# First feed-forward feature pair in plain products for both token halves, with split weight parts stored once and loaded for the second half

## The chip, the cores and the metric

The kernel runs on one core of a Trainium2 chip. The metric is the device time of one execution in microseconds. The kernel before takes 2255.2 us (median of three runs, 2255.18 to 2257.11).

## The reference

One decoder layer on 1024 tokens of 1024 features, in fp32: an mLSTM and a differential attention side by side, then cross-attention into 256 memory tokens, then a SwiGLU feed-forward with 2816 hidden features. Each sub-layer ends in x <- LayerNorm(alpha * x + f(x)). The change touches the end of the second sub-layer and the start of the third:

```python
    p = jax.nn.softmax(s, axis=-1)
    xo = jnp.einsum('bhqk,bkhd->bqhd', p.astype(xv.dtype), xv).reshape(B, S, XA_HEADS * XA_DHEAD)
    x = layer_norm(ALPHA * x + xo @ w_xo[l], ln2_g[l], ln2_b[l])

    hid = jax.nn.silu(x @ w_ffn_gate[l]) * (x @ w_ffn_up[l])
    x = layer_norm(ALPHA * x + hid @ w_ffn_down[l], ln3_g[l], ln3_b[l])
```

## The kernel before, in words

**Products.** Every fp32 operand is split into a high part (`whi`) and a remainder (`wlo`), and each product is three matmuls, high by high, high by low, low by high (`mm3`). A weight comes by DMA on SP's queue into `wraw` (three buffers); a high part is then a copy by ScalarE (ACT) or GpSimd (POOL), a low part a subtraction by VectorE (DVE) or POOL (`split_w`). `whi` and `wlo` have four buffers each, so four parts of 128 by 512 stand ready at a time. `turn` decides the engine: without a plan high parts alternate between ACT and POOL, and of four low parts three go to DVE and one to POOL.

**Order.** `Weave` runs generators one quantum at a time, and TensorE's order is the order in which they are stepped (one quantum of the attention output or of a plain product is six matmuls of 256 columns, or a few more). Work that must wait for LayerNorm is put in a heap by `W.later` and comes due after so many quanta. The other engines' order comes from a scheduler that goes by priority: `tc.high_priority(offset=AHEAD)` lets weight loads and splits stand ahead of other work. Once set, each engine's order is fixed and it waits in order.

**The stretch of the change.** The attention output and its LayerNorm (`g_add`) run once for the first 512 tokens (h = 0) and once for the last 512 (h = 1). Each half goes through four column quarters b, and each quarter through two units u of 256 tokens; a unit is eight quanta. Each quarter loads 1 MB of weights (`vo_d[b]`, two loads) and splits it into four parts, in each half anew. At quarter 3 each token tile of 128 rows gets its LayerNorm; in h = 1 POOL takes half of the last two steps of it (`LN2_POOL`).

`to_blocks(h, p)` then transposes two token tiles into PSUM tiles `tp` (a pool of five banks, four needed at once) and makes from them the blocks `x2[h]` of the feed-forward's input: four plain blocks and three or four sums and differences, each with a high and a low part. The gate and up products of a pair of feature blocks (q) use seven half-size products in place of eight (`g_seven`, Strassen's scheme in Winograd's form), so they need the sums and differences of the input and also those of the weights (`tt` on DVE). For the first pair (q = 0) the token halves differ: h = 0 is done by `g_seven` on 256 columns, as soon as its blocks are there; h = 1 is done by `g_plain`, eight products from plain blocks, while `block_sums` makes its sums from the plain blocks. From q = 1 on both halves go together through `g_seven`.

Of the kernel before, what the change touches and what calls it, by code (L numbers as in the profile page):

```python
# [12 lines left out]
F = mybir.dt.float32  # L13
R = mybir.dt.float32r
# [9 lines left out]
KT = 8  # L24
# [92 lines left out]
def hybrid_layer(ctx: ExitStack, tc: tile.TileContext, a: dict, out: bass.AP):  # L117
# [86 lines left out]
    def g_tm(wsrc, nk, units, evac):  # L204

        w = []
        for g0 in range(0, nk, 4):
            gn = min(4, nk - g0)
            w += split_all(load_w(wsrc[:, g0:g0 + gn, :]), gn * 256)
# [35 lines left out]
    hT_d = dr.tile([2, 8, 128, 1024], F, name="hT_d")  # L245
    oT_d = dr.tile([8, 128, 1024], F, name="oT_d")
# [711 lines left out]
    def g_add(wsrc, act, h, b, gb, dst=None):  # L958
# [12 lines left out]
        yield from g_tm(wsrc, KT, half(act), ev)  # L971
# [78 lines left out]
    def to_blocks(h, p):  # L1050
# [32 lines left out]
    def block_sums(p, late):  # L1083

        c = slice(p * 128, p * 128 + 128)

        def part(n, i):
            return x2[1][i][n][:, :, c].bitcast(F)

        t, u = diff_tile(), diff_tile()  # L1090
        if late:
            tt(t, part(3, 0), part(0, 0), OP.subtract)
            tt(u, part(3, 1), part(0, 1), OP.subtract)
            tt(t, t, u, OP.add)
            put(1, 3, c, t, "g")
            return
        tt(t, part(2, 0), part(3, 0), OP.subtract)
        tt(u, part(2, 1), part(3, 1), OP.subtract)
        tt(t, t, u, OP.add)
        put(1, 5, c, t, "g")  # L1100
        tt(u, t, part(0, 0), OP.add)
        tt(u, u, part(0, 1), OP.add)
        put(1, 4, c, u, "g")
        t = diff_tile()
        tt(t, part(1, 0), u, OP.subtract)
        tt(t, t, part(1, 1), OP.add)
        put(1, 6, c, t, "v")

    def g_sums(late):
        for p in range(2):  # L1110
            block_sums(p, late)
        yield from ()
# [320 lines left out]
```

## Time and profile before

| | |
|---|---|
| median of three runs | 2255.2 us |
| profiled execution | 2254.51 us |
| its span in the trace | 2252.6 us |
| TensorE busy | 2192.5 us (97%) |
| VectorE busy | 1386.7 us (62%) |
| ScalarE, GpSimd busy | 695.2 us, 709.7 us |
| HBM read, written | 168.92 MB, 41.98 MB |

The trace's times are microseconds from the span's start. A matmul's busy time is longer than the distance to the next one, since matmuls are pipelined: what counts is where one group starts and the next one starts. In brackets behind a row stands how long its engine was idle before it and what ended that. PEclk is TensorE's granted clock, 1.00 for 2.4 GHz and 0.50 for 1.2 GHz, as a mean over the stretch.

### The profile page before, as it was taken

How to read it: one execution, taken by the hardware profiler on the slowest of the kernel's cores; microseconds unless marked ns; L12 is line 12 of the kernel's file. 1: busy time of each engine (PE TensorE's matmuls, PEld its weight loads, DVE VectorE, ACT ScalarE, POOL GpSimd, SP SyncE). 2: the span in 40 equal slices, each digit the busy share in tenths (PEclk: the TensorE clock that was granted, in tenths of full speed). 3: DMA queues.
4: the chain of work that ended last, by engine and by line, in shares of the span. 5: the costliest groups of instructions: out<-in, count | busy, mean ns of one | idle time of the engine just before them, and what ended most of it. 6: DMA issues, size and time to landing. Idle time of an engine off the chain costs nothing.

```text
span 2252.6 us, 34100 instructions
## 1 busy us (share of the span) xinstructions
PE 2192.5 (97%) x13149; PEld 1953.5 (87%) x13149; DVE 1386.7 (62%) x2494; ACT 695.2 (31%) x1395; POOL 709.7 (32%) x723
## 2 busy tenths in 40 slices
PE   8999999999999999998999999997999999999997
PEld 8898898888898988886888999997888888888886
DVE  8536545314777777765535586478756666565667
ACT  3323223213555555555212123222211111111122
POOL 7124323203334343434422232245421121111223
PEclk9999999999999999999999999999999999999999
DMA  9322212334434454338653423222211111111122
GB/s 323 102 75 94 75 66 94 117 110 120 117 93 140 124 148 129 101 117 287 215 178 122 178 85 104 83 83 70 66 40 55 50 45 57 57 57 39 56 80 80
DMA packets 97953, 238.33 MB, mean 106 GB/s; under 512 B 12128, under 2 KB 30464, under 8 KB 97792
## 3 DMA queue, kind: packets, MB, share of 16 engines
q1 hardware_dynamic: 97792, 236.16, 32.1%
q8 instruction: 104, 1.70, 0.3%
q14 instruction: 57, 0.47, 0.1%
HBM read 168.92 MB, written 41.98 MB: 94 GB/s over the span
## 4 chain that ended last, share of the span: by engine, by line
PE 45%; DVE 4%; POOL 1%; issue 1%; ACT 0%; DMA 0%; DVEq 0%; POOLq 0%; ACTq 0%
PE acc L153 27%; PE xb L153 7%; PE xa L153 5%; PE xc L153 5%; DVE wlo L150 1%; DVE d L1039 1%; DVE z L929 0%; DVE z L925 0%; PE tp L1002 0%; DVE wraw L1039 0%; DVE u L1039 0%; DVE lst L935 0%; DVE xb L150 0%; PE tp L953 0%; DVE hidl L150 0%
## 5 line engine op out<-in xcount | busy, mean ns | idle before, releaser
L153 PE MATMUL acc<-bh,whi 128*128 128x512 f32 x2048 | 649.3, 398 | 0.4 <-ACT gtok L392 0.4
L142 POOL TENSOR_SCALAR whi<-wraw 128x512 fp32r<-128x512 f32 (+1 forms) x250 | 180.9, 724 | 889.2 <-issue 382.7
L153 PEld LDWEIGHTS acc<-bh,whi 128*128 128x128 f32 x2048 | 372.2, 188 | 65.7 <-ACT gtok L392 0.6
L150 DVE TENSOR_TENSOR wlo<-wraw,whi 128x512 fp32r<-128x512 f32 (+1 forms) x379 | 310.4, 823 | 189.9 <-ACT whi L140 148.8
L153 PE MATMUL acc<-bh,wlo 128*128 128x512 f32 x1024 | 400.3, 391 | 0.0
L140 ACT ACTIVATE whi<-wraw 128x512 fp32r<-128x512 f32 (+1 forms) x252 | 157.3, 625 | 553.5 <-PE acc L153 279.8
L153 PE MATMUL acc<-whi,bh 128*128 128x256 f32 (+1 forms) x1456 | 288.1, 288 | 0.2 <-DVE ev L150 0.2
L153 PEld LDWEIGHTS acc<-whi,bh 128*128 128x128 f32 x1456 | 234.2, 191 | 1.5 <-DVE ev L150 0.4
L153 PEld LDWEIGHTS acc<-bh,wlo 128*128 128x128 f32 x1024 | 192.3, 188 | 42.1
L153 PE MATMUL acc<-wlo,bh 128*128 128x256 f32 (+1 forms) x728 | 205.5, 282 | 0.0
L153 PE MATMUL xb<-xe,whi 128*128 128x256 f32 x1008 | 183.7, 282 | 10.7 <-DVE u L1039 7.8
L150 POOL TENSOR_TENSOR wlo<-wraw,whi 128x512 fp32r<-128x512 f32 (+1 forms) x125 | 174.6, 1397 | 10.3
L153 PEld LDWEIGHTS xb<-xe,whi 128*128 128x128 f32 x1008 | 160.3, 190 | 15.9 <-issue 6.7
L153 PE MATMUL xb<-xe,wlo 128*128 128x256 f32 x504 | 142.7, 283 | 0.0
L153 PEld LDWEIGHTS acc<-wlo,bh 128*128 128x128 f32 x728 | 138.8, 191 | 1.1
L1254 DVE SCALAR_TENSOR_TENSOR z<-z,acc 128x512 f32<-128x512 f32 x144 | 98.3, 685 | 53.7 <-PE acc L153 52.5
L153 PE MATMUL acc<-wlo,hidh 128*128 128x512 f32 x320 | 124.8, 390 | 1.4 <-DVE wlo L150 1.4
L153 PE MATMUL acc<-whi,hidh 128*128 128x512 f32 x320 | 124.6, 389 | 1.2 <-POOL whi L142 1.2
L153 PE MATMUL acc<-whi,hidl 128*128 128x512 f32 x320 | 124.7, 390 | 0.0
L688 ACT ACTIVATE e<-e,mx 128x256 f32<-128x256 f32 (+7 forms) x128 | 99.2, 775 | 73.5 <-DVE mx L683 71.8
L153 PE MATMUL xa<-xb,whi 128*128 128x512 f32 (+1 forms) x352 | 106.6, 386 | 5.3 <-ACT u L1166 5.3
L153 PE MATMUL xc<-xb,whi 128*128 128x512 f32 (+1 forms) x352 | 105.8, 383 | 1.6 <-DVE u L1039 1.6
(297 smaller groups left out, 4344.7 us busy)
## 6 DMA issues: line engine op xcount, KB each, us to landing
wraw<-in_wfm_dram SPq DMA_DIRECT2D x48, 512.0 KB, 3.5
wraw<-in_wg_dram SPq DMA_DIRECT2D x24, 512.0 KB, 3.5
wraw<-in_wu_dram SPq DMA_DIRECT2D x24, 512.0 KB, 3.5
wraw<-in_wd_dram SPq DMA_DIRECT2D x22, 512.0 KB, 3.5
hT_d<-hp SPq DMA_DIRECT2D x16, 512.0 KB, 2.8
g_d<-gt SPq DMA_DIRECT2D x32, 256.0 KB, 2.1
K<-rot SPq DMA_DIRECT2D x64, 128.0 KB, 2.4
klo<-raw SPq DMA_DIRECT2D x64, 128.0 KB, 2.4
```

What stands on the lines that cost most here:

```text
L140: S.activation(dst, src, AF.Copy)
L142: G.tensor_scalar(dst, src, 1.0, 0.0, op0=OP.mult, op1=OP.add)
L150: (V if eng == "v" else G).tensor_tensor(dst, src, hi.bitcast(F), op=OP.subtract)
L153: PE.matmul(o, l, r, start=start, stop=stop, skip_group_check=True)
L688: S.activation(e[c][:, :n], e[c][:, :n], AF.Exp, scale=-1.0, bias=mx[:, c:c + 1], accum_out=su[:, c:c + 1])
L1039: V.tensor_tensor(dst, x_, y_, op=op)
L1254: V.scalar_tensor_tensor(zs, zs, ALPHA if q == 0 else 1.0, acc, op0=OP.mult, op1=OP.add)
```

## The change

The attention output's first half stores the split parts of its weights to memory (`vs_d`), and its second half loads these parts straight into `whi` and `wlo`; it splits nothing. For q = 0 both token halves now use `g_plain`: h = 0 splits the weights and stores the parts (`pl_d`), h = 1 loads them. `to_blocks` makes six of the seven blocks for either half; while the plain products run, block 6 holds a plain block, and `g_sums` puts the seventh sum there when they are done. In this whole stretch all high parts of weights are made by ACT (`turn["plan"] = ("s", None)`).

```diff
-    def g_tm(wsrc, nk, units, evac):
-
-        w = []
-        for g0 in range(0, nk, 4):
-            gn = min(4, nk - g0)
-            w += split_all(load_w(wsrc[:, g0:g0 + gn, :]), gn * 256)
+    def load_parts(src):
+
+        hi = wp.tile([128, 512], R, tag="whi", name="whi", bufs=4)
+        lo = wp.tile([128, 512], R, tag="wlo", name="wlo", bufs=4)
+        with tc.high_priority(offset=AHEAD):
+            dma(hi.bitcast(F), src[0])
+            dma(lo.bitcast(F), src[1])
+        return hi, lo
+
+    def g_tm(wsrc, nk, units, evac, parts=None, again=False):
+
+        if again:
+            w = [load_parts(parts[i]) for i in range(4)]
+        else:
+            w = []
+            for g0 in range(0, nk, 4):
+                gn = min(4, nk - g0)
+                w += split_all(load_w(wsrc[:, g0:g0 + gn, :]), gn * 256)
+            if parts is not None:
+                for d, pair in zip(parts, w):
+                    for j in range(2):
+                        dma(d[j], pair[j].bitcast(F))
...
-        if h == 1:
-            for n, b in enumerate((b11, b21, b22, b12)):
-                put(1, n, c, b, "v")
-            return
-        put(0, 0, c, b11, "v")
-        t1 = diff_tile()
+        for n, b in ((0, b11), (1, b21)):
+            put(h, n, c, b, "v")
+        t1, t3 = diff_tile(), diff_tile()
         S.activation(t1, b12, AF.Copy)
-        t3 = diff_tile()
+        put(h, 6, c, b12, "v")
+        put(h, 2, c, b22, "v")
         tt(t3, b22, t1, OP.subtract)
         tt(t1, t1, b11, OP.subtract)
-        put(0, 5, c, t3, "g")
-        put(0, 1, c, b21, "v")
-        put(0, 3, c, t1, "g")
+        put(h, 5, c, t3, "g")
         t2 = diff_tile()
         tt(t2, b22, t1, OP.subtract)
-        put(0, 2, c, b22, "v")
-        put(0, 4, c, t2, "g")
-        t4 = diff_tile()
-        tt(t4, b21, t2, OP.subtract)
-        put(0, 6, c, t4, "g")
...
+        put(h, 3, c, t1, "g")
+        put(h, 4, c, t2, "g")
+
+    def g_sums(h):
...
+            t, u = diff_tile(), diff_tile()
+            tt(t, part(1, 0), part(4, 0), OP.subtract)
+            tt(u, part(1, 1), part(4, 1), OP.subtract)
             tt(t, t, u, OP.add)
-            put(1, 3, c, t, "g")
...
+            put(h, 6, c, t, "g")
         yield from ()
 
     gb2 = ln_rows(1)
+    turn["plan"] = ("s", None)
...
-    def g_plain(wsrc, f, up):
-
-        w = split_all(load_w(wsrc[f]))
+    def g_plain(wsrc, f, up, h):
+
+        kept = pl_d[2 * up + f]
+        if h == 0:
+            w = split_all(load_w(wsrc[f]))
+            for d, pair in zip(kept, w):
+                for j in range(2):
+                    dma(d[j], pair[j].bitcast(F))
+        else:
+            w = [load_parts(d) for d in kept]
...
-    W.add("g", g_gate_up(0, [0], False))
-    W.add("u", g_gate_up(0, [0], True))
-    W.add("g", g_plain(a["wg"], 0, False))
-    W.add("g", g_plain(a["wg"], 1, False))
-    W.add("s", g_sums(False))
-    W.add("u", g_plain(a["wu"], 0, True))
-    W.add("u", g_plain(a["wu"], 1, True))
-    W.add("s", g_sums(True))
+    for h in range(2):
+        for up in range(2):
+            for f in range(2):
+                W.add("p", g_plain(a["wu" if up else "wg"], f, up, h))
+        W.add("s", g_sums(h))
+    W.drain()
+    turn["plan"] = None
```

The first place is SP's queue from the attention output on. In the kernel before it holds the 16 loads of `vo_d` (both halves) and then loads of feed-forward weights:

```order
L167 DMA wraw<-vo_d 128x1024 x16
L167 DMA wraw<-in_wg_dram 128x1024 x2
L167 DMA wraw<-in_wu_dram 128x1024 x2
L167 DMA wraw<-in_wg_dram 128x1024 x2
L167 DMA wraw<-in_wu_dram 128x1024 x2
```

In the changed kernel the first half's loads stand among the stores of the parts, of which this is a stretch (`vs_83` and `vs_84` are parts 0 and 1 of quarter 2):

```order
L167 DMA wraw<-vo_d 128x1024
L225 DMA vs_83<-whi 128x512
L225 DMA vs_83<-wlo 128x512
L225 DMA vs_84<-whi 128x512
L167 DMA wraw<-vo_d 128x1024
L225 DMA vs_84<-wlo 128x512
```

The second half's queue then starts like this (`vs_75` to `vs_78` are the four parts of quarter 0):

```order
L167 DMA wraw<-in_wg_dram 128x1024
L167 DMA wraw<-in_wu_dram 128x1024
L210 DMA wlo<-vs_75 128x512
L209 DMA whi<-vs_75 128x512
L209 DMA whi<-vs_76 128x512
L210 DMA wlo<-vs_76 128x512
L209 DMA whi<-vs_77 128x512
L210 DMA wlo<-vs_77 128x512
```

A store of a part stands behind the split that makes it, a load of a part waits until TensorE has done with the part that has held its buffer, and what stands behind either on SP waits too. Eight loads of 256 KB take the place of two of 512 KB in each quarter of the second half.

The second place is DVE where the last token tile (`z7`) has its LayerNorm and the last blocks are made. In the kernel before:

```order
L925 SCALAR_TENSOR_TENSOR z7_12157<-z7_12157,lmv_15753,lng_14578 128x512 x2
L929 SCALAR_TENSOR_TENSOR z7_12157<-z7_12157,lrs_15759,lnb_14579 128x512
L150 TENSOR_TENSOR wlo_16116<-wraw_16113,whi_16115 128x512
L150 TENSOR_TENSOR wlo_16120<-wraw_16113,whi_16119 128x512
L150 TENSOR_TENSOR hidl_15773<-sg_15854,hidh_15772 128x2x128
L150 TENSOR_TENSOR xb_14576<-tp_15977,xb_14574 128x4x128
L1039 TENSOR_TENSOR u3_16035<-xb_15950,u1_15964 128x256
L150 TENSOR_TENSOR xb_14576<-tp_15987,xb_14574 128x4x128
L1039 TENSOR_TENSOR u3_16035<-xc_15951,u3_16035 128x256
L150 TENSOR_TENSOR xb_14576<-tp_15982,xb_14574 128x4x128
L1039 TENSOR_TENSOR u3_15868<-u3_15868,u3_16035 128x256
```

And in the changed kernel:

```order
L943 SCALAR_TENSOR_TENSOR z7_12181<-z7_12181,lmv_15789,lng_14602 128x512 x2
L150 TENSOR_TENSOR wlo_16050<-wraw_16047,whi_16049 128x512
L947 SCALAR_TENSOR_TENSOR z7_12181<-z7_12181,lrs_15795,lnb_14603 128x512
L150 TENSOR_TENSOR wlo_16054<-wraw_16047,whi_16053 128x512
L1057 TENSOR_TENSOR s1_16424<-wraw_16422 128x512
L150 TENSOR_TENSOR xb_14600<-tp_15961,xb_14598 128x4x128
L150 TENSOR_TENSOR xb_14600<-tp_15966,xb_14598 128x4x128
L1057 TENSOR_TENSOR wraw_16422<-wraw_16420,wraw_16422 128x512
L150 TENSOR_TENSOR xe_15807<-tp_15971,xe_15806 128x4x128
L150 TENSOR_TENSOR xb_14600<-tp_15976,xb_14598 128x4x128
L1057 TENSOR_TENSOR d_15986<-tp_15976,d_15985 128x512
L1057 TENSOR_TENSOR d_15985<-d_15985,tp_15961 128x512
```

The combining of the seven products (`u1` to `u3`) is gone from between the blocks. The row that ends the fence is the last reader of the first transposed tile `tp_15961`; until then that tile's PSUM bank is taken.

The third place is TensorE in the last plain call of h = 0, with the transposes of tiles 6 and 7, one quantum into the call:

```order
L153 MATMUL acc<-xb,whi 128x256 x2
L153 MATMUL acc<-xb,wlo 128x256
L153 MATMUL acc<-xe,whi 128x256 x2
L153 MATMUL acc<-xe,wlo 128x256
L1076 MATMUL tp<-ident,z_12180 128x128 x8
L1076 MATMUL tp<-ident,z_12181 128x128 x8
L153 MATMUL acc<-xb,whi 128x256 x2
```

The transposes of tiles 4 and 5 stand one quantum into the call before. In the kernel before both pairs of tiles come among the seven-product calls.

## Rows read from the trace of the kernel before

**Rows 1.** The page's first part: busy time, share of the span, instructions.
```profile
PE 2192.5 (97%) x13149; PEld 1953.5 (87%) x13149; DVE 1386.7 (62%) x2494; ACT 695.2 (31%) x1395; POOL 709.7 (32%) x723
```

**Rows 2.** Windows: length, busy us (instructions) by engine, granted clock, DMA share, GB/s.
```profile
1544.20:1551.80 7.60, 6.04 (x37) 5.85 (x37) 6.06 (x10) 0.05 (x1) 5.72 (x6) 0.78 0.44 140
1560.90:1570.60 9.70, 3.11 (x25) 2.94 (x25) 9.70 (x15) 1.05 (x2) 8.17 (x7) 0.89 0.44 155
1570.60:1577.47 6.87, 6.87 (x40) 6.87 (x41) 6.29 (x13) 3.44 (x6) 0.00 (x0) 0.66 0.04 13
1577.47:1600.51 23.04, 23.04 (x194) 23.04 (x193) 22.77 (x29) 7.70 (x14) 11.90 (x9) 1.00 0.21 69
1600.51:1611.53 11.02, 5.75 (x38) 5.05 (x36) 9.83 (x12) 2.27 (x4) 7.20 (x6) 0.90 0.01 1
1611.53:1616.53 5.00, 5.00 (x13) 3.96 (x13) 2.89 (x4) 0.00 (x0) 1.46 (x3) 0.53 0.06 8
```

**Rows 3.** TensorE's timeline: start, length, operation, idle before it and its releaser.
```profile
1536.89 0.40 PE L153 MATMUL xa<-xb,whi 128*128 128x256 f32 x2
...
1544.20 0.52 PE L153 MATMUL xb<-xe,whi 128*128 128x256 f32 x2 [2.86 <-POOL whi L142]
...
1570.60 0.76 PE L153 MATMUL xb<-xe,whi 128*128 128x256 f32 x2 [6.56 <-DVE u L1039]
1572.01 3.48 PE L1058 MATMUL tp<-ident,z 128*128 128x128 f32 x16
...
1600.51 0.63 PE L153 MATMUL xa<-xb,whi 128*128 128x512 f32 x2
...
1611.53 1.22 PE L153 MATMUL xa<-xb,whi 128*128 128x512 f32 x2 [5.27 <-ACT u L1166]
...
1627.73 0.39 PE L153 MATMUL acc<-whi,hidh 128*128 128x512 f32 x1
```

**Rows 4.** TensorE's timeline: sixteen transposes and what follows them.
```profile
1502.03 1.91 PE L1058 MATMUL tp<-ident,z 128*128 128x128 f32 x16
1503.69 0.36 PE L153 MATMUL acc<-whi,pt 128*128 128x256 f32 x1
```

**Rows 5.** The chain of waits in order of time: two products of a seven-product call.
```profile
1616.69 2.84 PE xb L153 x24
1619.53 2.76 PE xc L153 x12
```

**Rows 6.** TensorE's timeline: gaps in the attention output's second half.
```profile
1497.65 0.39 PE L153 MATMUL acc<-wlo,pt 128*128 128x256 f32 x1 [0.62 <-DVE wlo L150]
...
1511.49 0.63 PE L1058 MATMUL tp<-ident,z 128*128 128x128 f32 x4 [0.50 <-DVE xb L150]
```

**Rows 7.** DVE's instructions by form, 1538.2 to 1627.7: busy us, mean ns, idle before.
```profile
L150 DVE TENSOR_TENSOR wlo<-wraw,whi 128x512 fp32r<-128x512 f32 x20 | 17.5, 881 | 5.4 <-POOL whi L142 3.3 <-ACT whi L140 2.1
L150 DVE TENSOR_TENSOR xb<-tp,xb 128x512 fp32r<-128x512 f32 x8 | 5.4, 674 | 0.3 <-ACT xb L140 0.2
L964 DVE SCALAR_TENSOR_TENSOR z<-z,acc 128x256 f32<-128x256 f32 x2 | 0.7, 364 | 0.0
L936 DVE BATCH_NORM_AGGREGATE lmv<-lst 128x2 f32<-128x12 f32 x3 | 0.6, 198 | 0.0
```

**Rows 8.** POOL's instructions by form, 1531 to 1570.
```profile
L945 POOL TENSOR_TENSOR z<-z,lnb 128x512 f32<-128x512 f32 x4 | 5.7, 1436 | 0.3
L944 POOL TENSOR_SCALAR z<-z,lrs 128x512 f32<-128x512 f32 x4 | 5.4, 1362 | 2.3 <-DVE z L925 2.3
L920 POOL TENSOR_TENSOR lrs<-lsc,mhalf 128x1 f32<-128x1 f32 x4 | 4.0, 990 | 11.9 <-DVE lsc L938 11.9
```

**Rows 9.** DMA issues: count, KB each, median us from issue to landing.
```profile
bh<-hT_d SPq DMA_DIRECT2D x16, 512.0 KB, 7.4
wraw<-vo_d SPq DMA_DIRECT2D x16, 512.0 KB, 3.7
```

**Rows 10.** SP's timeline: eight of the `hT_d` loads.
```profile
1042.00 7.76 SPq L820 DMA_DIRECT2D bh<-hT_d  x8
```

**Rows 11.** Windows: the ten us that hold these loads, columns as in the second group.
```profile
1042.00:1052.00 10.00, 6.75 (x27) 5.46 (x26) 4.93 (x14) 5.43 (x12) 2.92 (x4) 0.83 1.05 397
```

More of the change, by code (lines that the diff above doesn't have):

```diff
@@ L245, in hybrid_layer @@
     hT_d = dr.tile([2, 8, 128, 1024], F, name="hT_d")
+    vs_d = [[dr.tile([2, 128, 512], F, name=f"vs{b}{i}") for i in range(4)] for b in range(4)]
+    pl_d = [[dr.tile([2, 128, 512], F, name=f"pl{b}{i}") for i in range(2)] for b in range(4)]
     oT_d = dr.tile([8, 128, 1024], F, name="oT_d")
@@ L956, in to_feature, with g_add @@
             to_lo(dst[1][:, 4 * g:4 * g + 4, c], t3, dst[0][:, 4 * g:4 * g + 4, c], "v")
-    def g_add(wsrc, act, h, b, gb, dst=None):
+    def g_add(wsrc, act, h, b, gb, dst=None, parts=None):
         def ev(u, acc):
@@ L970, in ev @@
                         W.later(LAG_B[u] if h else LAG_B0, lambda: to_blocks(h, u))
-        yield from g_tm(wsrc, KT, half(act), ev)
+        yield from g_tm(wsrc, KT, half(act), ev, parts, parts is not None and h == 1)
     gb1 = ln_rows(0)
@@ L1109, in g_sums, with part @@
-    def g_sums(late):
-        for p in range(2):
-            block_sums(p, late)
+        put(h, 3, c, t1, "g")
+        put(h, 4, c, t2, "g")
+    def g_sums(h):
+        for p in range(2):
+            c = slice(p * 128, p * 128 + 128)
+            def part(n, i):
+                return x2[h][i][n][:, :, c].bitcast(F)
+            t, u = diff_tile(), diff_tile()
+            tt(t, part(1, 0), part(4, 0), OP.subtract)
+            tt(u, part(1, 1), part(4, 1), OP.subtract)
+            tt(t, t, u, OP.add)
+            put(h, 6, c, t, "g")
@@ L1112, in g_sums @@
         yield from ()
     gb2 = ln_rows(1)
+    turn["plan"] = ("s", None)
     for b in range(4):
-        W.add(f"o0{b}", g_add(vo_d[b], pT[0], 0, b, gb2))
+        W.add(f"o0{b}", g_add(vo_d[b], pT[0], 0, b, gb2, None, vs_d[b]))
     W.drain()
     for b in range(4):
-        W.add(f"o1{b}", g_add(vo_d[b], pT[1], 1, b, gb2))
+        W.add(f"o1{b}", g_add(vo_d[b], pT[1], 1, b, gb2, None, vs_d[b]))
     W.drain()
@@ L1220, in g_plain @@
             for t in range(2):
-                n = ((0, 3), (1, 2))[k // 4][t]
+                n = ((0, 6), (1, 2))[k // 4][t]
                 mm3(acc[:, t * 256:(t + 1) * 256], cut(w[k // 4], (k % 4) * 128, (k % 4) * 128 + 128),
-                    (x2[1][0][n][:, k % 4, :], x2[1][1][n][:, k % 4, :]), k + t == 0, k == 7)
+                    (x2[h][0][n][:, k % 4, :], x2[h][1][n][:, k % 4, :]), k + t == 0, k == 7)
             yield
-        if not up:
-            sg[f] = temp("sg")
-            S.activation(sg[f], acc, AF.Silu)
-            return
-        st = sg[f]
-        tt(st, st, acc, OP.mult)
-        s4 = st.rearrange("p (t q r) -> p t q r", t=2, r=128)
-        d = [x_[:, f, 512:].rearrange("p (q t r) -> p t q r", t=2, r=128) for x_ in hid]
-        to_hi(d[0], s4, "g")
-        to_lo(d[1], s4, d[0], "v")
+        with tc.high_priority(offset=AHEAD_U):
+            if not up:
+                sg[f] = temp("sg")
+                S.activation(sg[f], acc, AF.Silu)
+                return
+            st = sg[f]
+            tt(st, st, acc, OP.mult)
+            s4 = st.rearrange("p (t q r) -> p t q r", t=2, r=128)
+            d = [x_[:, f, h * 512:h * 512 + 512].rearrange("p (q t r) -> p t q r", t=2, r=128) for x_ in hid]
+            to_hi(d[0], s4, "s")
+            to_lo(d[1], s4, d[0], "v")
     def down_w(q):
```

20 lines of the change are left out of this document (removed).

## The prediction

> **What bounds the kernel now.** I read the page's busy times first. TensorE is busy 97% of the span [rows 1], so a gain can only come from places where it stands still, runs slowly or does work that can go. A list of its idle gaps then shows the large ones in one place, the start of the feed-forward: TensorE's timeline there has it idle for 2.86, 6.56 and 5.27 us at a time [rows 3], with smaller gaps between, and the windows show after each of the large ones a granted clock below 1.00 (0.78, 0.66 and 0.53 as a mean, so partly at 1.2 GHz) while it is busy again [rows 2]. In the same windows DVE is busy 9.70 of 9.70, 22.77 of 23.04 and 9.83 of 11.02 us [rows 2]. TensorE waits for DVE, or for ACT and POOL work that DVE feeds. So this stretch is bound by VectorE, and only there does DVE work cost time.
>
> How much is lost is measured against TensorE's own pace. In the plain products of h = 1, without a gap, 192 matmuls of 256 columns (four calls of 48) go by in the 23.04 us from 1577.47 to 1600.51 [rows 2, 3], which is 0.120 us each. Sixteen transposes take 1503.69 - 1502.03 = 1.66 us [rows 4]. A product of 512 columns in a seven-product call takes 2.76 us, and 2.84 where it is cut into 256-column pieces [rows 5].
>
> The first pair before (1536.89 to 1600.51): 63.62 us [rows 3]. Its work is 2 x 84 matmuls for h = 0 (seven products, four k, three matmuls) and 192 for h = 1, 360 x 0.120 = 43.2 us, and 2 x 1.66 us of transposes: 46.5 us. So 17.1 us are lost.
> The next gate call (1600.51 to 1627.73): 27.22 us [rows 3] for 4 x 2.76 + 3 x 2.84 = 19.6 us of work: 7.6 us lost, through the 5.27 us gap and the slow clock after it.
> The attention output's second half loses 0.62 + 0.50 = 1.1 us in its two gaps [rows 6].
>
> **The change part by part.**
>
> TensorE's work grows. Both halves need 192 plain matmuls, 384 x 0.120 = 46.1 us, with the transposes 49.4 us in place of 46.5: 2.9 us more, and this lies fully on the path.
>
> DVE's work shrinks. A 512-column operation takes 0.674 us and a 256-column one 0.364 us when nothing disturbs it [rows 7]. In the attention output's second half 16 low parts go, three of four from DVE: 12 x 0.674, 8 us. In the first pair two calls of seven products go: two weight combinations of four operations each (5.4 us), 14 low parts, ten or eleven of them DVE's (7.1 us), ten operations that combine products (3.6 us) and eight that make the four 256-column results of the up call (2.9 us). Two more up evictions of two operations come (2.7 us); the plain splits stay eight, since h = 1 loads its parts. That is 16 us less, and the blocks take 20 operations a pair of tiles in place of 22 over both halves, 2.7 us less. With 19 us less in a stretch where DVE was full, it need not hold TensorE all along. If the losses vanish altogether, the gain is 63.6 - 49.4 = 14.2 us in the first pair, 7.6 in the next gate call and 1.1 in the attention output: 22.9 us. That is the ceiling.
>
> Residual wait at the last blocks. In the new order tiles 4 and 5 are transposed 17 quanta into the first pair and tiles 6 and 7 after 25. Counted from the end of the first unit of quarter 3 (5.76 us, 48 x 0.120, ahead of the first pair), TensorE reaches the latter at 5.76 + 25 x 0.72 + 1.66 = 25.4 us, and after four transposes, 0.4 us, needs a PSUM bank that the first pair of tiles still holds (five banks, four used) until DVE has done the last row of the second place shown. Up to that row DVE has 32 operations of 512 columns at about 0.68 us [rows 7] and 12 short ones (four at 0.364, four at 0.198, four below): 21.8 + 3.0 = 24.8 us. POOL works beside it nearly all that time (four LayerNorm halves at 1.436 + 1.362 and 0.990 [rows 8], 15 us, and two low parts), and two-input DVE operations were longer beside POOL: a low part took 0.881 us as a mean against 0.674 for one from PSUM [rows 7], 30% more, which would make it 32 us. So the wait is between 25.8 - 24.8, below zero, thus nothing, and 32 - 25.8 = 6 us. At the far end, if DVE is no earlier than now, the transposes come 1572.01 - 1536.89 = 35.1 us after the first pair's start [rows 3] where they now want 19.7: 15 us. I take 3 us, the middle of the nearer two ends, and 1 us for a slower clock after it (after the 2.86 us gap, 7.60 us ran at 0.78 [rows 2], 0.22 x 7.60 = 1.7 us lost). What stands behind: ACT waits in order at the block that goes where the LayerNorm's rows lie until POOL has done tile 7, and with it the eviction of the first up product; its accumulator is needed two calls later, so that is covered by 5 us and more.
>
> The parts' loads in the attention output's second half. A part is freed in unit 1 of a quarter after its two quanta and is wanted again in unit 0 of the next; for each of the four parts that is 5.76 - 1.44 = 4.32 us later. What fills it now is a split on ACT and DVE from a weight that is there already; then it is two DMAs of 256 KB. A 512 KB load from the same scratch lands 3.7 us after its issue [rows 9], and SP's second issue comes some 0.4 us later: 4.1 us against 4.32. The next pair is asked for 1.44 us later, 0.52 MB in 1.44 us or 364 GB/s while it lasts, and eight `hT_d` loads of 512 KB with the same 2 KB rows, issued one after another in 7.76 us [rows 10], ran at 397 GB/s [rows 11]. So they just fit. Bounds: nothing, since 4.1 is below 4.32, and, if each pair lands as the `hT_d` loads did in the median, 7.4 us [rows 9], 3.1 us in each of four quarters, 12.3 us. I take 0.3 us a quarter, 1.2 us, being nearest to the 3.7 us row.
>
> The Trainium skill speaks against such small transfers. Its page "DMA: Bandwidth & Descriptors", section Bandwidth, advises to batch transfers to 1 MiB or more for three quarters of the peak, and gives 358 GB/s as a core's limit from HBM. The trace differs in both: 512 KB transfers in a row ran at 397 GB/s [rows 11]. By that limit of the Trainium skill's page a quarter's 2.1 MB would take an estimated 5.9 us where they are asked for in 5.76, 0.1 us more a quarter, and the sum would be 2237.4.
>
> The rest costs nothing here. The second half of q = 0 loads its parts with a ring of four buffers, each part freed 2.88 us into a call and its buffer wanted two calls later, 2 x 5.76 - 2.88 = 8.64 us, twice the time above. The 32 and 16 stores (256 KB each) stand on SP ahead of later weight loads; each waits for a split that TensorE needs anyway some us later, and the weight loads behind are needed a quarter (11.5 us) or a call (5.76 us) later. High parts go from POOL to ACT, which was busy 7.70 of 23.04 us [rows 2]; without that cover a high part costs 0.6 us once per quarter. The seventh sums come while the next gate call runs its first five products (some 14 us), on a DVE that is then free.
>
> Sum, against the profiled execution: 22.9 - 4 - 1.2 = 17.7 us off 2254.5 gives 2236.8; the median of the runs shown lies 0.7 us above that execution, so 2237 to 2238. I forecast 2237.
>
> **The rivals.**
> 1. The blocks of h = 1 stay late. LayerNorm, blocks and POOL work for h = 1 are untouched and now stand right before the plain products of h = 1, which need them at once; before, the whole of h = 0's seven products lay between. For it: POOL's 15 us and DVE's order. Against: 19 us less on DVE. If half of the 15 us above is waited, 7.5 with 2 us of clock, in place of 4: 2237 + 5.5 = 2243; with all 15 us and 3 of clock, 2251.
> 2. Slower: the parts' loads go one after another. SP has one queue, each load waits for a buffer, and if each pair takes its 3.7 us alone [rows 9], four need 14.8 us from 7.2 us into a quarter, 22.0; the last is wanted at 11.52 + 4.32 = 15.8. That is 6.2 us a quarter, 25 in four, and 1.7 us of clock each, 32 in place of 1.2: 2237 + 31 = 2268. It decides from about 4.5 us per quarter on, which eats the 18 us. Against it stands the 397 GB/s of eight loads in a row [rows 11]. The Trainium skill's page "DMA: Bandwidth & Descriptors" (section Bandwidth) leads the same way with its advice against small transfers; the rows so far are against it.
> 3. The loads overlap but land as late as the `hT_d` median: 12.3 us and some clock, 2237 + 12 = 2249 to 2252.
> 4. Nothing waits: the ceiling, 2254.5 - 22.9 + 0.7 = 2232.
>
> **How the numbers follow.** Forecast (2234 to 2241) 0.50; rival 1 0.22; rival 4 0.13; rival 3 0.08; rival 2 0.07. A measurement of this kernel tells 0.2% (4.5 us) from no change. Faster by more than that is below 2250.7: the forecast, rival 4, nearly all of rival 1 and half of rival 3, 0.89. Within: 0.05. Slower: most of rival 2, 0.06. The range from 2231 (the ceiling with a little more) to 2250 leaves out rival 2 and the ends of 1 and 3, and holds some 0.85.
>
> **What would show it.** In the profile after, the first pair should start within 1.5 us of 1536.9 and take some 53 us from its first matmul to the first of q = 1, with DVE no longer at 95% and more; the gap of 6.56 us and the 5.27 us gap should be gone, and the next gate call should take under 21 us. A wait of some 3 us should stand at the transposes of tiles 6 and 7, released by a DVE block operation. In the attention output's second half gaps released by loads of parts should sum to about 1 us and the DMA rate should be about twice what it was. I am wrong if such gaps reach several us per quarter, if the first plain call of h = 1 waits for blocks by more than 5 us, or if the time lies above 2250.

## The result, and the profile after

The changed kernel takes 2231.8 us (median of four runs, 2231.03 to 2232.62) against 2255.45 us for the kernel before on the same chip (2255.18 to 2257.11): ratio 0.9896, 95% interval 0.9885 to 0.9908. The forecast was 2237 us, the range 2231 to 2250. The profiled execution takes 2231.29 us, its span is 2229.3 us.

The page's first part, answering [rows 1]:

```profile
PE 2187.3 (98%) x13173; PEld 1950.3 (87%) x13173; DVE 1343.7 (60%) x2446; ACT 695.7 (31%) x1392; POOL 677.6 (30%) x688
```

TensorE executes 24 matmuls more and is busy 5.2 us less, since less of its work runs at the slow clock; and it stands idle for 42.0 us of the span in place of 60.1.

TensorE's timeline at the first pair, answering [rows 3] (start, length, operation, idle before it and its releaser):

```profile
1537.78 0.40 PE L153 MATMUL acc<-xb,whi 128*128 128x256 f32 x2
...
1557.36 1.47 PE L1076 MATMUL tp<-ident,z 128*128 128x128 f32 x12
...
1559.76 0.63 PE L1076 MATMUL tp<-ident,z 128*128 128x128 f32 x4 [0.93 <-DVE d L1057]
...
1566.09 0.39 PE L153 MATMUL acc<-xe,whi 128*128 128x256 f32 x1 [0.23 <-DVE xe L150]
...
1588.75 0.63 PE L153 MATMUL xa<-xb,whi 128*128 128x512 f32 x2
...
1608.30 0.39 PE L153 MATMUL acc<-whi,hidh 128*128 128x512 f32 x1
```

The first pair takes 1588.75 - 1537.78 = 50.97 us (before 63.62), the gate call behind it 1608.30 - 1588.75 = 19.55 us (before 27.22). Of the gaps of 2.86, 6.56 and 5.27 us none is left; the two waits above, 1.16 us in sum, are all of more than 0.15 us in the two stages.

The windows of the same stretch, answering [rows 2], same columns; the first is the attention output's second half:

```profile
1490.00:1537.78 47.78, 46.58 (x387) 45.93 (x386) 26.31 (x51) 10.80 (x19) 12.13 (x11) 1.00 0.46 150
1537.78:1549.90 12.12, 12.12 (x105) 12.12 (x103) 12.09 (x24) 5.06 (x8) 10.41 (x9) 1.00 0.89 282
1549.90:1557.36 7.46, 7.46 (x67) 7.46 (x65) 7.46 (x9) 3.14 (x6) 4.67 (x4) 1.00 0.87 297
1557.36:1566.09 8.73, 7.56 (x64) 7.15 (x63) 6.65 (x11) 4.92 (x9) 3.83 (x3) 1.00 0.48 172
1566.09:1588.75 22.66, 22.66 (x188) 22.66 (x189) 15.94 (x22) 7.20 (x12) 10.27 (x8) 1.00 0.36 116
1588.75:1608.30 19.55, 19.55 (x123) 17.53 (x121) 10.04 (x14) 5.20 (x9) 6.59 (x7) 1.00 0.18 55
```

VectorE is still full, 12.09 of 12.12 and 7.46 of 7.46 us, at the start of the pair, but TensorE is busy all of these 19.58 us: of what VectorE makes there, its plain products need only the low parts of weights (the transposes at 1549.90, of tiles 4 and 5, need the LayerNorm of these). Over the whole pair VectorE is busy 42.14 of 50.97 us (the sum of the four rows of the pair). The kernel before, over its pair:

```profile
1536.89:1600.51 63.62, 51.37 (x394) 50.52 (x393) 59.46 (x89) 20.64 (x38) 36.85 (x31) 0.92 0.20 67
```

So VectorE has 17.3 us less to do in the pair. The granted clock is 1.00 in all six rows after.

Where the 23.3 us of span come from, each stage from its marks in TensorE's timeline:

| stage (us) | before | after | gain |
|---|---|---|---|
| attention output, both halves | 98.60 | 98.93 | -0.33 |
| first pair | 63.62 | 50.97 | 12.65 |
| gate call of q = 1 | 27.22 | 19.55 | 7.67 |
| from there to the last down products | 566.74 | 566.75 | -0.01 |
| last down products | 48.46 | 45.36 | 3.10 |
| behind the last matmul | 9.67 | 8.89 | 0.78 |

The rest, -0.6, is ahead of the attention output. The last two lines, 3.9 us together, stand in no term of the prediction: they lie 570 us behind the change. TensorE before, where the last down products begin:

```profile
2197.86 0.51 PE L153 MATMUL acc<-whi,hidh 128*128 128x512 f32 x1 [1.19 <-POOL whi L142]
2199.78 0.75 PE L153 MATMUL acc<-wlo,hidh 128*128 128x512 f32 x1 [1.42 <-DVE wlo L150]
```

and after:

```profile
2178.87 0.50 PE L153 MATMUL acc<-wlo,hidh 128*128 128x512 f32 x1 [1.39 <-POOL wlo L150]
```

One wait of 1.39 us in place of two with 2.61. The windows of the 39.5 us behind them show the rest, a granted clock of 0.96 before

```profile
2200.50:2240.00 39.50, 39.50 (x170) 32.57 (x169) 28.24 (x76) 12.22 (x19) 15.87 (x20) 0.96 0.20 76
```

and 1.00 after:

```profile
2179.50:2219.00 39.50, 39.50 (x176) 32.72 (x175) 29.92 (x81) 12.95 (x20) 16.45 (x21) 1.00 0.20 77
```

The same length of time holds 176 and not 170 matmuls. The wait of 1.42 us comes from VectorE's order before:

```profile
2195.55 1.78 DVE L150 TENSOR_TENSOR xe<-wraw,xe 128x512 fp32r<-128x512 f32 x1
2197.25 1.09 DVE L1039 TENSOR_TENSOR u<-u,u 128x512 f32<-128x512 f32 x1
2198.26 0.68 DVE L1039 TENSOR_TENSOR u<-xc,u 128x512 f32<-128x512 f32 x1
2198.86 0.87 DVE L150 TENSOR_TENSOR wlo<-wraw,whi 128x512 fp32r<-128x512 f32 x1
```

The low part that TensorE needs stands behind two sums of the last up products. In the changed kernel POOL makes it.

### The profile page after: what moved, and what is told of

It reads as the page before. It is cut to its first block, busy times and chain, and to the rows that moved or that the text cites. A ratio compares the mean times of both kernels' runs of the same rounds, so it can differ in the third digit from the quotient of the medians.

```text
span 2229.3 us, 34179 instructions
## 1 busy us (share of the span) xinstructions
PE 2187.3 (98%) x13173; PEld 1950.3 (87%) x13173; DVE 1343.7 (60%) x2446; ACT 695.7 (31%) x1392; POOL 677.6 (30%) x688
## 4 chain that ended last, share of the span: by engine, by line
PE 47%; DVE 2%; DMA 1%; issue 0%; POOL 0%; ACT 0%; SPq 0%; DVEq 0%; POOLq 0%; ACTq 0%
PE acc L153 29%; PE xb L153 8%; PE xc L153 5%; PE xa L153 5%; DMA wlo<-vs 1%; DVE z L947 0%; PE tp L1020 0%; DVE z L943 0%; PE tp L971 0%; DVE wlo L150 0%; PE tp L1076 0%; DVE xb L150 0%; DVE lst L953 0%; DVE s L1057 0%; POOL wlo L150 0%
## 5 line engine op out<-in xcount | busy, mean ns | idle before, releaser
L142 POOL TENSOR_SCALAR whi<-wraw 128x512 fp32r<-128x512 f32 (+1 forms) x224 | 160.8, 718 | 842.8 <-issue 334.9
L150 DVE TENSOR_TENSOR wlo<-wraw,whi 128x512 fp32r<-128x512 f32 (+1 forms) x358 | 286.0, 803 | 192.7 <-ACT whi L140 154.2
L150 POOL TENSOR_TENSOR wlo<-wraw,whi 128x512 fp32r<-128x512 f32 (+1 forms) x118 | 165.7, 1404 | 50.4 <-ACT whi L140 41.2
L153 PE MATMUL xb<-xe,whi 128*128 128x256 f32 x960 | 173.0, 280 | 0.0
L153 PEld LDWEIGHTS xb<-xe,whi 128*128 128x128 f32 x960 | 151.7, 188 | 4.7
L153 PE MATMUL xb<-xe,wlo 128*128 128x256 f32 x480 | 135.1, 281 | 0.0
L153 PE MATMUL xc<-xb,whi 128*128 128x512 f32 x320 | 99.3, 391 | 0.0
L153 PE MATMUL xa<-xb,whi 128*128 128x512 f32 x320 | 98.9, 390 | 0.0
```

The costliest lines, as they stand in the source:

```text
L142: G.tensor_scalar(dst, src, 1.0, 0.0, op0=OP.mult, op1=OP.add)
L150: (V if eng == "v" else G).tensor_tensor(dst, src, hi.bitcast(F), op=OP.subtract)
L153: PE.matmul(o, l, r, start=start, stop=stop, skip_group_check=True)
```

## The experiments

Twelve kernels in three batches, each batch on one chip with the kernel before beside it (2254.73, 2255.5 and 2255.8 us). Profiled executions differ by up to 4 us already ahead of the attention output, so below 2 us I go by stages. `turn["h"]` and `turn["l"]` count the splits and decide whose turn the next one is; where an experiment changes their number, the line `turn["h"], turn["l"] = 0, 2` ahead of the last down weights sets the counters to what the changed kernel has there (its own values, taken as turns). In the expectations theory D says that the first pair is bound by VectorE and that relieving it is the gain; theory R says that the gain at the end of the kernel comes from shifted turns.

**Which part of the change it is.** The feed-forward part alone (high parts by ACT now from the first pair on):

```diff
-    turn["plan"] = ("s", None)
...
-        W.add(f"o0{b}", g_add(vo_d[b], pT[0], 0, b, gb2, None, vs_d[b]))
+        W.add(f"o0{b}", g_add(vo_d[b], pT[0], 0, b, gb2))
...
-        W.add(f"o1{b}", g_add(vo_d[b], pT[1], 1, b, gb2, None, vs_d[b]))
+        W.add(f"o1{b}", g_add(vo_d[b], pT[1], 1, b, gb2))
...
+    turn["plan"] = ("s", None)
```

> The changed kernel without its attention-output part: both halves split the weights anew and nothing is stored; the feed-forward part stays, with its stored parts, and the counters at the end are those of the changed kernel. Theory D (VectorE held TensorE only after the attention output, so what is saved inside it brings nothing): 2231 to 2234. Rival (the 8 us of VectorE and the POOL work saved in the second half let its LayerNorm and blocks start earlier, and that is part of the gain): 2236 to 2242.

Measured 2229.6 us (0.9889, 0.9874 to 0.9904); first pair 50.96, gate call 19.54, attention output 97.44. The time is below both expectations: all of the gain is there, and the attention output is 1.5 us shorter than with the stored parts. The attention-output part alone, in the kernel before (the helpers that store and load, as in the change, are left out here):

```diff
...
-        W.add(f"o0{b}", g_add(vo_d[b], pT[0], 0, b, gb2))
+        W.add(f"o0{b}", g_add(vo_d[b], pT[0], 0, b, gb2, None, vs_d[b]))
...
-        W.add(f"o1{b}", g_add(vo_d[b], pT[1], 1, b, gb2))
+        W.add(f"o1{b}", g_add(vo_d[b], pT[1], 1, b, gb2, None, vs_d[b]))
```

> The kernel before with the attention-output part alone (stored parts, high parts by ACT); first pair as before, counters at the end as in the changed kernel. Theory D: like the kernel before with the new counters, 2250 to 2252.5. Rival: 2244 to 2249.

Measured 2249.58 us (0.9981, 0.9972 to 0.9991), with the pair at 63.34 and the gate call at 27.08 us as before. It has the changed counters, and with these alone (below) the kernel before takes 2250.92 us. So this part brings nothing that these times tell from nothing; its attention output takes 99.12 us (98.60 before). The time lies between the two expectations. No stored part at all: to the edit of the feed-forward run comes

```diff
-        if h == 0:
-            w = split_all(load_w(wsrc[f]))
...
-        else:
-            w = [load_parts(d) for d in kept]
+        w = split_all(load_w(wsrc[f]))
```

> The changed kernel without any stored part: attention output splits anew in both halves, and so do the plain calls. What is left of the change is that both halves' first feature pair runs in plain products, with seven or fewer blocks a half due ahead of them. Theory D with the attention part worth nothing: the sum of the run without the attention part (2229.6) and of what the plain splits cost (0 to 3 us): 2229.5 to 2233. Rival (stored parts are needed for the plain order to pay): 2238 or more, with DVE full through the whole pair.

Measured 2231.3 us (0.9897, 0.9882 to 0.9912), the first expectation. The pair takes 50.16 us, less than with stored parts, and VectorE is still busy 16.3 us less in it than in the kernel before:

```profile
1536.64:1586.80 50.16, 49.62 (x419) 49.40 (x418) 43.17 (x67) 23.57 (x42) 30.45 (x24) 1.00 0.26 85
```

The gate call takes 21.42 us, more, through one wait for ACT's copy of the first product. Ahead of this copy in ACT's order stand a block of the seventh sums, for which ACT first waits 4.57 us until VectorE has its sum, a hidden block and a high part:

```profile
1594.15 0.72 PE L153 MATMUL xa<-xb,whi 128*128 128x512 f32 x2 [1.61 <-ACT u L1161]
```

The same with the attention output's stored parts left in (only the edit just shown):

> The changed kernel, but the second half's four plain calls load the raw weights and split them anew, and nothing of them is stored. Theory D (DVE is full from 1537.8 to 1557.4, 19.6 of 19.6 us, so any operation put there delays the blocks that the transposes of tiles 6 and 7 wait for): 4 of the 8 low parts fall to DVE at 0.7 to 0.9 us each, two of them into the full stretch, so the pair stage takes 52 to 54 us instead of 51.0 and the time is 2232.5 to 2234.5. Rival (the second half's calls have slack, DVE 15.9 of 22.7 us, and the stored parts are not needed): pair stage within 0.5 us of 51.0, time 2231 to 2232.

Measured 2233.15 us (0.9906, 0.9892 to 0.9919). That is within the time of theory D, but not by its reason: the pair is 50.17 us, with no wait at the transposes (one of 0.54 us for a low part), and the gate call has the same 1.61 us wait (21.42 us). VectorE's timeline without stored parts shows why the low part that now stands ahead of the last blocks costs nothing there:

```profile
1555.48 0.68 DVE L1057 TENSOR_TENSOR d<-tp,d 128x512 f32<-128x512 f32 x1
1556.08 0.68 DVE L150 TENSOR_TENSOR wlo<-wraw,whi 128x512 fp32r<-128x512 f32 x1
1556.67 0.68 DVE L1057 TENSOR_TENSOR d<-d,tp 128x512 f32<-128x512 f32 x1
...
1581.64 0.68 DVE L1057 TENSOR_TENSOR s<-wraw 128x512 f32<-128x512 f32 x1
1582.36 0.69 DVE L1057 TENSOR_TENSOR wraw<-wraw 128x512 f32<-128x512 f32 x1
```

The two sums of the next gate call's weights (`s`, `wraw`), which the changed kernel does ahead of these blocks, went some 28 us back: their weights are loaded only from 1570.23 on (1544.65 in the changed kernel), behind the raw weights of the second half's plain calls, which need the same three buffers. So the wait left the pair and came up in the gate call.

By stages, the stored parts of the plain calls are worth 1.1 us (pair and gate call together 70.5 us with them and 71.6 without, in both comparisons), and those of the attention output cost 1.5 us there. The 20 us are those of plain products for both halves. These bring several things at once: TensorE has work that doesn't wait for the late blocks, VectorE has 16 to 17 us less to do in the pair, and POOL makes no high parts of their weights. No run parts them. The next one shows that the order alone is not enough.

**What bounds the pair.** Work put back on VectorE (16 low parts of the first half's plain calls made over again), without any other edit to the pair:

```diff
-            w = split_all(load_w(wsrc[f]))
+            raw = load_w(wsrc[f])
+            w = split_all(raw)
+            with tc.high_priority(offset=AHEAD):
+                for j, pair in enumerate(w):
+                    for _ in range(2):
+                        to_lo(pair[1], raw[:, j * 512:j * 512 + 512], pair[0], "v")
```

> The changed kernel with 16 low-part subtractions of the first half's plain calls done twice more on DVE (values unchanged, about 0.88 us each, 14 us of DVE work). Theory D (the pair is bounded by DVE's blocks, which is what the change relieved): what does not fit into DVE's idle time ahead of the pair comes back as waits at the transposes of tiles 6 and 7, pair stage 57 to 63 us, time 2237 to 2244. Rival (the gain came from the order of TensorE's calls alone, DVE has room): pair stage within 1 us of 51.0, time 2231 to 2233.

Measured 2244.63 us (0.9955, 0.9942 to 0.9969), a pair of 64.34 us, 13.4 longer, both a little more than theory D had. VectorE is busy 51.29 us in it, 9.15 more than in the changed kernel. Eleven low parts run in one go there from 1539.29 on, 8.21 us, ahead of the LayerNorm of the last tiles, and POOL's half of the LayerNorm is late with it. TensorE's waits of more than 0.2 us sum to 9.9 us, 8.7 more than in the changed kernel; 7.7 of them are at the transposes, now of both pairs of tiles, and 2.2 at low parts:

```profile
1555.74 0.66 PE L1076 MATMUL tp<-ident,z 128*128 128x128 f32 x4 [1.25 <-POOL z L963]
...
1563.09 0.39 PE L153 MATMUL acc<-xb,wlo 128*128 128x256 f32 x1 [1.45 <-DVE lsc L956]
...
1567.62 1.09 PE L1076 MATMUL tp<-ident,z 128*128 128x128 f32 x4 [3.36 <-POOL z L963]
...
1570.21 1.08 PE L1076 MATMUL tp<-ident,z 128*128 128x128 f32 x4 [1.50 <-DVE xe L150]
...
1572.60 1.08 PE L1076 MATMUL tp<-ident,z 128*128 128x128 f32 x4 [1.30 <-DVE d L1057]
```

The remaining 4.6 of the 13.4 us go with the clock, 0.92 where the changed kernel has 1.00:

```profile
1539.11:1603.45 64.34, 54.45 (x418) 52.42 (x417) 51.29 (x79) 20.89 (x34) 30.30 (x23) 0.92 0.46 156
```

So VectorE work that is put ahead of the LayerNorm and the last blocks costs about its own length, and the clock on top: with the plain order too, VectorE's time up to the last block is the bound, and the changed kernel has little room left in it. The rival, the order alone, falls.

One thing stays open. In the kernel before, VectorE itself waits for POOL where the first gaps are:

```profile
1541.71 0.69 DVE L150 TENSOR_TENSOR wlo<-wraw,whi 128x512 fp32r<-128x512 f32 x1 [1.77 <-POOL whi L142]
...
1549.50 0.69 DVE L150 TENSOR_TENSOR wlo<-wraw,whi 128x512 fp32r<-128x512 f32 x1 [1.54 <-POOL whi L142]
```

POOL makes the first of these high parts behind its half of a LayerNorm, and the gap of 2.86 us ends with another. All runs with plain products for both halves also have the weights' high parts on ACT. What that alone would do for the kernel before was not run.

**How tight the loads are.** Each part in two transfers, cut by columns:

```diff
-            dma(hi.bitcast(F), src[0])
-            dma(lo.bitcast(F), src[1])
+            for t, d in ((hi, src[0]), (lo, src[1])):
+                for c in (slice(0, 256), slice(256, 512)):
+                    dma(t[:, c].bitcast(F), d[:, c])
```

> The changed kernel with each stored part loaded in two transfers of 128 KB instead of one of 256 KB, so four instead of two for a pair of parts. If a load has to land within the 4.32 us that one group of four products of the attention output leaves it, and the number of transfers on the SP queue sets when it lands, the two waits for low parts (0.20 and 0.96 us) grow to 3 to 6 us in sum: 2233 to 2237. If the bytes set it, the halves land as the wholes did: waits within 1 us of before, 2231 to 2232.5.

Measured 2250.76 us (0.998, 0.9972 to 0.9989): 19 us lost, more than either expectation. In the profile the attention output takes 117.79 us, 18.86 more than in the changed kernel: 13.7 us of it are waits, the rest goes with a granted clock of 0.90 from the first of them on. TensorE waits once in each quarter of the second half:

```profile
1488.16 0.58 PE L153 MATMUL acc<-wlo,pt 128*128 128x256 f32 x1 [3.99 <-DMA wlo<-vs]
...
1507.56 0.58 PE L153 MATMUL acc<-wlo,pt 128*128 128x256 f32 x1 [5.12 <-DMA wlo<-vs]
...
1525.36 0.38 PE L153 MATMUL acc<-wlo,pt 128*128 128x256 f32 x1 [1.07 <-DMA wlo<-vs]
...
1541.80 0.58 PE L153 MATMUL acc<-wlo,pt 128*128 128x256 f32 x1 [4.68 <-DMA wlo<-vs]
```

The transfers themselves are quick (median 2.6 and 2.9 us to landing, below the 3.5 and 3.8 us of the whole parts). The same cut by partitions, with the rows as long as in the changed kernel:

```diff
-                for c in (slice(0, 256), slice(256, 512)):
-                    dma(t[:, c].bitcast(F), d[:, c])
+                for c in (slice(0, 64), slice(64, 128)):
+                    dma(t[c, :].bitcast(F), d[c, :])
```

> The changed kernel with each stored part loaded in two transfers of 128 KB as in the last run, but cut by partitions (64 rows of 2 KB) and not by columns (128 rows of 1 KB). If the smaller rows made that run 19 us longer (its rate was 237 to 273 GB/s in the busy slices where 256 KB transfers showed up to 378), this one stays within 3 us of the changed kernel: 2231 to 2235. If the number of transfers did (each takes 0.32 to 0.42 us of the SP queue's issue, 8 more a call), it is 2244 to 2252 again.

Measured 2267.24 us (1.0057, 1.0042 to 1.0072): both expectations fell. The rows' length isn't it, and the same number of transfers cost twice as much. TensorE now waits twice a quarter; the waits for high parts are

```profile
1489.33 0.54 PE L153 MATMUL acc<-whi,pt 128*128 128x256 f32 x1 [3.95 <-DMA whi<-vs]
...
1512.07 0.35 PE L153 MATMUL acc<-whi,pt 128*128 128x256 f32 x1 [3.94 <-issue]
...
1534.63 0.38 PE L153 MATMUL acc<-whi,pt 128*128 128x256 f32 x1 [1.30 <-DMA whi<-vs]
...
1556.63 0.35 PE L153 MATMUL acc<-whi,pt 128*128 128x256 f32 x1 [3.94 <-issue]
```

with 4.11, 4.31, 3.73 and 4.05 us for low parts behind them. What differs is the order on SP's queue that the scheduler chose. In the run cut by columns these rows stand near the end of quarter 1's loads (`vs10` to `vs13` are its four parts; each row is half a part, `x2` both halves; two more halves of low parts follow):

```
L211 DMA whi_15336<-vs13_82 128x256 x2
L211 DMA wlo_15337<-vs13_82 128x256
L211 DMA wlo_15325<-vs11_80 128x256
L211 DMA wlo_15319<-vs10_79 128x256
```

and these near the end of quarter 2's (one more half follows):

```
L211 DMA wlo_15533<-vs21_84 128x256
L211 DMA wlo_15527<-vs20_83 128x256
L211 DMA wlo_15539<-vs22_85 128x256
L211 DMA wlo_15545<-vs23_86 128x256
L211 DMA whi_15544<-vs23_86 128x256 x2
```

In quarter 1, as in 0 and 3, half of part 0's low part (`vs10`) stands behind loads into the buffers of part 3, which come free only when the quarter before has ended, and part 0 is what TensorE wants next: 3.99, 5.12 and 4.68 us. In quarter 2 it (`vs20`) stands ahead of them: 1.07 us. In the run cut by partitions the same holds for part 0's high part (behind part 3 in quarters 0, 1 and 3: 3.95, 3.94, 3.94; ahead in quarter 2: 1.30), and its low part is behind part 3 in all four. All twelve waits agree with the place in the queue. That it is the cause is argued from this: a run that changes this order and nothing else was not made. The changed kernel has both loads of part 0 first in every quarter, and waits twice, which answers to [rows 6]:

```profile
1499.62 0.39 PE L153 MATMUL acc<-wlo,pt 128*128 128x256 f32 x1 [0.20 <-DMA wlo<-vs]
...
1529.16 0.38 PE L153 MATMUL acc<-wlo,pt 128*128 128x256 f32 x1 [0.96 <-DMA wlo<-vs]
```

with these loads, answering [rows 9]:

```profile
wlo<-vs SPq DMA_DIRECT2D x16, 256.0 KB, 3.8
whi<-vs SPq DMA_DIRECT2D x16, 256.0 KB, 3.5
```

Both parts in one transfer of 512 KB:

```diff
-        hi = wp.tile([128, 512], R, tag="whi", name="whi", bufs=4)
-        lo = wp.tile([128, 512], R, tag="wlo", name="wlo", bufs=4)
+        t = wp.tile([128, 2, 512], R, tag="wpair", name="wpair", bufs=4)
         with tc.high_priority(offset=AHEAD):
-            dma(hi.bitcast(F), src[0])
-            dma(lo.bitcast(F), src[1])
+            dma(t.bitcast(F), src.rearrange("a p c -> p a c"))
```

> The changed kernel with the high and the low part of a stored pair in one tile, stored and loaded by one transfer of 512 KB in rows of 2 KB: half as many transfers. If the number of transfers sets when parts land, the two waits (0.20 and 0.96 us) go: 2230 to 2231.5. If the bytes and their rows do, the high part now lands with the low one, later than it did, and the waits grow to 1 to 4 us in sum: 2232 to 2236.

Measured 2233.81 us (0.9905, 0.9889 to 0.9922). A pair now lands in 4.5 us as a median, and the waits for parts are 0.34, 0.63 and 0.93, 1.90 us in sum, as the second expectation has it. The wait at the last transposes also grew, from 0.93 to 2.74 us. VectorE's timeline shows it:

```profile
1558.09 0.77 DVE L1057 TENSOR_TENSOR s<-wraw 128x512 f32<-128x512 f32 x1 [1.78 <-DMA wraw<-in_wg_dram]
1558.79 0.68 DVE L1057 TENSOR_TENSOR d<-d,tp 128x512 f32<-128x512 f32 x1
```

The weight sum of the next gate call stands here between the last two block operations and waits 1.78 us for its weights, and the operation that frees the PSUM bank waits behind it. By stages this cost more than the 2 us between the medians: 0.9 us in the attention output, 2.9 in the pair (53.83 us; the clock was 0.89 in the 15 us behind the wait) and 2.3 in the last down products (47.69 us), which wait 0.57 and 1.27 us and then run at 0.96. The profiled execution was 2.8 us ahead of that of the changed kernel before all this, so the sum can't be compared with the medians more closely.

**The end of the kernel.** First the kernel before with the changed kernel's counters:

```diff
         raw = [load_w(a["wd"][2 * NQ - 4 + f]) for f in range(4)]
+        turn["h"], turn["l"] = 0, 2
```

> The kernel before with the counters set at the same place to the values of the changed kernel. Theory R: 2251 to 2252.5, with one gap of 1.4 us at the last group. Rival: 2255.

Measured 2250.92 us (0.998, 0.9971 to 0.999). The last down products take 45.45 us in place of 48.46, with waits of 0.81 and 0.21 us and a clock of 1.00. Then the changed kernel with the counters of before:

```diff
+        turn["h"], turn["l"] = 0, 0
```

> The changed kernel, but the counters that rotate weight splits among engines are set, before the last down weights are split, to the values they have there in the kernel before. Theory R (about 3.9 us of the gain come from the end of the kernel, where the change has shifted this rotation by two): the gap before the last group of down products opens again to about 2.6 us with a slow clock behind it, and the time is 2235 to 2236. Rival (the end is faster for another reason, such as an earlier start or the clock): 2231 to 2233.

Measured 2230.94 us (0.9894, 0.9877 to 0.991): the loss does not come back, the last down products take 45.53 us. The same engines make the same parts as in the kernel before, but VectorE's order is another:

```profile
2176.21 1.77 DVE L150 TENSOR_TENSOR xe<-wraw,xe 128x512 fp32r<-128x512 f32 x1
2178.49 0.87 DVE L150 TENSOR_TENSOR wlo<-wraw,whi 128x512 fp32r<-128x512 f32 x1 [0.51 <-POOL whi L142]
2179.29 0.95 DVE L150 TENSOR_TENSOR xb<-u,xb 128x256 fp32r<-128x256 f32 x2
2180.16 0.68 DVE L1057 TENSOR_TENSOR u<-xc,u 128x512 f32<-128x512 f32 x1
```

Here the low part stands ahead of the sum of `xc`, there behind it. So shifted turns are enough to remove the wait, but they are not needed: theory R holds for the order of the kernel before and falls for that of the changed one. It hangs on where the scheduler puts one subtraction.

**A faster version.** The feed-forward run with the second tile pair's transposes two quanta later:

```diff
-LAG_B = (25, 25)
+LAG_B = (25, 27)
```

> The kernel without the attention-output part (2229.6) with the transposes of the second half's second tile pair due two slots later (27 for 25). The wait of 0.9 us at the last transposes and its 0.2 us at the block after it go if only DVE's lateness makes them; if a slot is cheaper than the wait, 2228 to 2229.3. Rival: the blocks, two slots later, are late for the products that read them: 2230 to 2233.

Measured 2229.05 us (0.9887, 0.9872 to 0.9901), the time expected, but not for its reason; the 0.6 us to the run without the later slots can't be told from nothing. The wait only moved: 0.53 and 0.57 us at the first products that read the new blocks, and the pair takes 50.98 us as ever. And with the last weights on ACT and DVE:

```diff
-PLAN_L = (("s", "v"), None)
+PLAN_L = (("s", "v"), ("s", "v"))
```

> The same with the last down weights' splits all on ACT and DVE (the second of the two plans there, until now POOL's turns), so that the low part that POOL delivers 1.4 us late comes from DVE. If POOL's slowness (1.4 to 1.6 us for a low part against 0.7 to 0.9 on DVE) is the wait, the last group is 1 to 1.5 us shorter: 2227 to 2228.5. Rival: DVE has the sums of the other products there and the low part is late on it as well: within 0.5 us of the kernel with the later slots alone, or slower.

Measured 2229.01 us (2226.7 to 2229.62; 0.9884, 0.9869 to 0.9899). The wait is down from 1.41 to 0.26 us, and the last down products take 44.25 us in place of 45.39, as expected; what stands behind them takes 0.27 us more. By stages that is 0.9 us gained. It doesn't show in the times, 2229.05 and 2229.01 us, and the profiled span is 2227.2 us in both because this execution was 0.9 us later already ahead of the attention output. The three versions with stored parts in the feed-forward alone take 2229.0 to 2229.6 us and beat both kernels, the changed one by 2 to 3 us, though in other batches than its own.

## Why the prediction was right, and where it was off

**The ceiling and its mechanism: right in the main.** The work left was put at 49.4 us for the pair and 19.6 for the gate call; measured are 50.97 with 1.16 us of waits, and 19.55. The pair starts at 1537.78 (expected within 1.5 us of 1536.9). VectorE's work in the pair was put some 19 us lower and is 17.3 us lower. The run with work put back on VectorE shows the bound. What the reading left out is POOL: behind the gap of 2.86 us VectorE is busy only 6.06 of 7.60 us [rows 2], and it waits 3.3 us for high parts from POOL [rows 7], so at the first gaps VectorE was not alone the bound.

**The residual wait: mechanism right, size too large.** The step took 3 us and 1 us of clock; it is 0.93 + 0.23 us, and the granted clock stays at 1.00. It stands where it was put, at the transposes of tiles 6 and 7, released by the operation named. VectorE's timeline there:

```profile
1553.53 1.77 DVE L1057 TENSOR_TENSOR s<-wraw 128x512 f32<-128x512 f32 x1
...
1557.62 0.67 DVE L150 TENSOR_TENSOR xb<-tp,xb 128x512 fp32r<-128x512 f32 x1
1558.22 0.67 DVE L1057 TENSOR_TENSOR d<-tp,d 128x512 f32<-128x512 f32 x1
1558.93 0.69 DVE L1057 TENSOR_TENSOR d<-d,tp 128x512 f32<-128x512 f32 x1
```

The last row frees the bank at 1559.62, that is 1559.62 - (1537.78 - 5.76) = 27.6 us on the prediction's count, between its ends of 24.8 and 32. The 32 long and 12 short operations are there as counted, two weight sums among them, and took 11% longer than their undisturbed count, though single ones were stretched much more (1.77 us for a sum). TensorE came to the wait at 26.8 us, not 25.8: twelve transposes run ahead of it, not four, so the bank that is still held is wanted by the last of the four tiles. This term set the forecast 2.8 us too high. That the time, 2231.8 us, is that of rival 4 (2232), where nothing waits, and only 0.8 us above the lower end of the range, is no sign for that rival: TensorE did wait, and 3.9 us came from a place that no rival has.

**VectorE "no longer at 95% and more": right for the pair as a whole, wrong where it counts.** It is busy 42.14 of 50.97 us (83%; before 59.46 of 63.62, 93%), but 99.8% of the first 19.58. The step equated less work with a free engine; VectorE is even fuller there than before (16.27 of the first 19.58 us then), and TensorE has other products for that time.

**The loads: size right, in part by luck; how near the edge they are was not seen.** 1.2 us were predicted as 0.3 in each of four quarters; measured are 0.20 and 0.96 in two of them, 1.16 us, at 150 GB/s in place of 79. With the same bytes in twice as many transfers and another order in the queue, the loss was 19 and 35 us. Rival 2 had 32 us, from loads that land one after another; in these runs they land quickly (2.6 to 2.9 us) but are issued late, behind loads that wait for a buffer.

**The attention output's saving: right that it would be little, wrong that it belonged in the sum.** The gaps there (1.1 us, and a third of 0.20 us that the prediction left out) went and came back as loads; without the stored parts the stage is shorter still (97.44 us).

**Not foreseen: 3.9 us at the end.** No step asked what a different number of splits does to the engines' turns and the scheduler's order 570 us later. Against the profiled execution the forecast was 5.5 us too high (2236.8 against 2231.29): 3.9 us from here and 2.8 from the residual wait, less 1.2 in small terms (the pair's own work 0.4, the attention output 0.2, 0.6 ahead of it). Measured against the kernel before with the changed counters (2250.92 us, another batch), the change itself is worth 19.1 us where 17.7 were forecast.

## What to carry to other kernels

Where one engine's work bounds a stretch, look for work of its consumer that doesn't need it, and for a form of the work that asks less of the bound engine: plain products in place of seven did both and gave 20 us here, though TensorE has more to do with them. Sparing VectorE its splits by stored parts gave 1.1 us in one place and cost 1.5 in the other. A change that shifts round-robin turns or a scheduler's order acts wherever a wait is balanced on one instruction, so compare every stage of the two traces, not only the edited one. In a queue that runs in order, look for transfers that stand behind one that waits for a buffer: the runs whose order had that lost 19 and 35 us, while doubling the size of the transfers added 0.7 us of waits for them.

## What the runs showed of the hardware

- Some short waits left the clock as it was: after 0.93 us at the transposes, 1.39 us at the last down products, and 0.88 and 0.40 us there (1.8 us from the start of the first to the end of the second), the granted clock stayed at 1.00. Waits of 1.19 and 1.42 us (within 3.1 us) were followed by 0.96 over 39.5 us, and 0.57 and 1.27 us (within 2.3 us) in the run with 512 KB transfers by 0.96 as well; there 2.74 us at the transposes were followed by 0.89 over the next 15 us. A pair with 9.9 us of waits ran at 0.92.
- Landing grew slower than size on SP's queue: 2.6 to 2.9 us for 128 KB, 3.5 to 3.8 for 256 KB, 4.5 for 512 KB (medians, in the attention output's second half).
